# Seven products of quarters in 44 of 76 projections of a two-layer hybrid trunk

## The chip, the cores and the metric

The kernel runs on one core of a Trainium2 chip. The metric is the device time of one execution in microseconds (us); lower is better. Before the change three runs gave 1742.62, 1742.88 and 1743.02 us.

## The reference

Two layers work on x of 512 tokens by 2048 features in float32. Each layer normalises x, projects it with one matrix `w_in` (2048 by 7696), feeds three branches with slices of the projection, and sends the concatenated branches through `w_out` (2048 by 2048) into the residual.

```python
h = _rmsnorm(x, norm_g)
proj = h @ w_in          # 4 x 512 conv, 4 x 1024 attention, 256+256+512+512+16 GLA
y_conv = b_gate * (conv3(c_gate * cv_h) + bias) * silu(cv_g)
# stick-breaking attention, 8 heads of 128, strictly causal
z = q @ k.T              # q, k RMS-normed per head
log_keep = where(mask, log_sigmoid(-z), 0)
later = cumsum(log_keep, reverse=True) - log_keep
w = where(mask, exp(log_sigmoid(z) + later), 0)
y_sb = (w @ v) * silu(sb_g)
# gated linear attention (GLA), 4 heads, decay per key feature
y_gla = _rmsnorm(o, gla_on_g) * silu(gl_g)
return x + concat([y_conv, y_sb, y_gla]) @ w_out
```

## The kernel before

**Products in three terms.** Float32 is carried by pairs of float16: every operand a is split into a high part, float16(a), and a low part, float16(a - high), after scaling by a power of two. A product is high x high + high x low + low x high, accumulated in PSUM. ScalarE (ACT) makes the high parts, VectorE (DVE) the low parts by one scalar-tensor-tensor instruction.

**Groups.** All weights are cut into 76 column groups of 256 (38 per layer; one has 16 columns more), listed in `specs` in the order in which they are used: six for GLA, four for the first half of the convolution, sixteen for attention (V, gate, Q, K for each of four pairs of heads), four for the second half of the convolution, eight for `w_out`. A group is 2048 rows by 256 columns: 16 blocks k of 128 rows.

- Token-major groups (`project_toks`, `tok_mm`, L576 to L578) hold a block of x (128 by 128) stationary and move 256 weight columns: 4 token blocks x 16 k x 3 terms = 192 matmuls. `project_by_token` (L601) does the same work, token block by token block.
- Column-major groups (`project_cols`, L568 to L570) hold 128 weight columns stationary and move 512 tokens: 2 x 16 x 3 = 96 matmuls.

**Weights.** `fetch` (L308) loads a group from DRAM on the SP queue as two staged halves of 1 MB, two groups ahead. Staging has three buffers of half a group. `load_` prepares the next group: a square with a sum on ACT (`wmax`, L319) for its scale, a reduction across partitions on GpSimd and a few tiny DVE instructions (`wscale`, L329 to L350), then the high half on ACT (`whi`, L392) and the low half on DVE (`wlo`, L399), each as two instructions of 2048 elements. For `w_out` a separate scale for each pair of rows makes that four instructions of 512 elements in each half.

**Mix.** Every branch output is split into a high and a low part with a scale of its own as soon as it exists (`mixsplit`, L647 and L648) and stays in SBUF until the output groups; the ratios of the scales are put into the `w_out` weights (`weight_ratio`).

**Attention.** While the projections of one pair of heads run, the scores and values of the pair before are put between them (`later`, `go`). `scores` makes for each head and each of two chunks of 896 and 384 elements: |z|, its exponential and ln(1+e) on ACT (L952 to L954), relu(-z) (L956), then on DVE w = -relu - ln (L958), a = z - w (L959), a reversed running sum of a (L962), w minus the shifted sum (L965), an exponential on ACT (L966), and the float16 pair of the result (L969, L970), which SP transposes by DMA. `values` multiplies by V (L988) and gates the result (L995). `gate` (L611 to L618) computes SiLU with five ACT instructions and two of DVE for each 512 tokens. Q and K are normalised and split by L1033 to L1054 and transposed by DMA.

**Output.** `finish` (L1078) adds the residual, stores the result, and ACT squares it for the next norm (L1084). The last output group goes token block by token block, and `xprep` makes the normalised x of the next layer behind it (L447 to L487).

What sets the order: each engine runs its own queue in order. The order on DVE and ACT at the start is written out by hand; the rest is ordered at build time from the program's order, with raised priority for the loading of weights. PSUM has three banks for projections (`psp`), two double banks for attention and GLA (`psz`) and one more (`psm`).

Of the kernel before, what the change touches and what calls it, by code (L numbers as in the profile page):

```python
# [20 lines left out]
XBITS = 8.0  # L21
# [9 lines left out]
CHUNKS = ((((3, 0), (2, 512)), (3, 2)), (((0, 0), (1, 128)), (0, 1)))  # L31


@with_exitstack
def hybrid_trunk(ctx, tc, x, norm_g, w_in, conv_w, conv_b, sb_qn_g, sb_kn_g,
# [10 lines left out]
    GX = GW + LR  # L46
    NG = D // GW
# [37 lines left out]
    xs = dram.tile([seq, D], F32, tag="xs", name="xs")  # L85
    xt = [newbig("x", [P, 2, D], F32) for _ in range(2)]
# [22 lines left out]
    parno = wk([P, 32], "raw", 1)  # L109
# [162 lines left out]
    specs = []  # L272
    for l in range(depth):
        for cols in ([(GL_V, GW)], [(GL_V + GW, GW), (GL_LR, LR)], [(GL_Q, GW)], [(GL_K, GW)],
                     [(GL_G, GW)], [(GL_G + GW, GW)]):
            specs.append((l, w_in, cols))
        conv = [[(l, w_in, [(c0 + j * GW, GW)]) for c0 in (CV_H, CV_C, CV_G, CV_B)] for j in range(2)]
        specs += conv[0]
        for j in range(4):
            for c0 in (SB_V, SB_G, SB_Q, SB_K):  # L280
                specs.append((l, w_in, [(c0 + j * GW, GW)]))
        specs += conv[1]
        for gi in range(NG):
            specs.append((l, w_out, [(gi * GW, GW)]))
# [10 lines left out]
    def junk(n):  # L295

        return wk([P, HK * GX], "junk", 1, dt=U8)[:, :n]


    def fetch(i):  # L300

        l, src, cols = specs[i]
        staged[i] = st = []
        for h in range(2):
            s_ = stage.tile([P, HK, GX], F32, tag="st", name=nm("st"))
            o = 0
            for c0, w in cols:
                nc.sync.dma_start(  # L308
                    s_[:, :, o:o + w],
                    src[l, h * HK * P:(h + 1) * HK * P, c0:c0 + w].rearrange("(k p) n -> p k n", p=P))  # L310
                o += w
            st.append(s_)

    def wmax(i, h):

        n = sum(c[1] for c in specs[i][2])
        if h == 0:
            peak[i] = sm(2, "wm")
        S.activation(junk(HK * n).rearrange("p (k n) -> p k n", k=HK), staged[i][h][:, :, :n], AF.Square,  # L319
                     accum_out=peak[i][:, h:h + 1])  # L320

    def wscale(i):

        l, src, cols = specs[i]

        m = sm(1, "wq")
        if i:
            gm = sm(2, "wgm")
            G.partition_all_reduce(gm, peak.pop(i), P, RED.add)  # L329
# [14 lines left out]
        sw = None  # L344
        if src is w_out:
            sw = sm(8, "wsr")
            V.tensor_scalar(sw, ratio[l][0], sc, None, ALU.mult)
            V.tensor_tensor(u, p2, ratio[l][1], ALU.mult)
        else:
            V.tensor_tensor(u, p2, xun[:, l:l + 1], ALU.mult)  # L350
        loaded[i] = ([], u)
        scales[i] = (sc, sw)

    def wparts(i, h):
        sc, sw = scales[i]
        return [(slice(2 * j, 2 * j + 2), sw[:, h * 4 + j:h * 4 + j + 1]) for j in range(4)] \
            if sw is not None else [(slice(0, HK), sc)]
# [13 lines left out]

    def whi0(h, q, eng):

        if q == 0:
            wh = wpool.tile([P, HK, GX], F16, tag="wh", name=nm("wh"))
            wl = wpool.tile([P, HK, GX], F16, tag="wl", name=nm("wl"))
            loaded[0][0].append((wh, wl))
# [751 lines left out]
```

## Time and profile before

| | |
|---|---|
| Median of three runs | 1742.88 us |
| Span of the profiled execution | 1740.9 us |
| TensorE matmuls busy | 1726.8 us, 12846 matmuls |
| TensorE weight loads busy | 1232.4 us |
| DVE busy | 1068.9 us, 2015 instructions |
| ACT busy | 1090.0 us, 1460 instructions |
| GpSimd (POOL) busy | 75.1 us, 104 instructions |
| DMA | 204.69 MB, mean 118 GB/s |
| Granted TensorE clock | 1.000 |

The span runs from the first to the last instruction; the execution's own time is not listed apart from the runs, and the span lies 2.0 us under their median. Matmuls overlap, so their busy time says when the engine had work and not how fast it ran; the pace is seen from one start to the next. A row of a group gives line, engine, operation, output and inputs with shapes and the count, then busy us and mean ns of one, then the engine's idle time ahead of these instructions and what ended it. The names in a row are those of the buffers' first users, so that a block of x may stand as `m`.

### The profile page before, as it was taken

What the parts mean: (1) busy time and instruction counts of PE and PEld (TensorE: products, weight loads), DVE (VectorE), ACT (ScalarE), POOL (GpSimd) and SP (SyncE); (2) the same over time, 40 slices, a digit from 0 to 9 for tenths busy, and PEclk for the clock granted to TensorE, in tenths of its full rate; (3) what the DMA queues carried; (4) which work ended last, traced back from release to release, by engine and by line L of the source; (5) the groups of instructions that cost most, each with busy time, mean ns of one, the idle gap of its engine ahead of it and who ended that gap; (6) DMA issues with size and microseconds to landing.
All of it is one profiled execution on the core that took longest, in us unless ns stands there. A gap on an engine that the chain in (4) does not pass through costs nothing.

```text
span 1740.9 us, 30651 instructions
## 1 busy us (share of the span) xinstructions
PE 1726.8 (99%) x12846; PEld 1232.4 (71%) x12846; DVE 1068.9 (61%) x2015; ACT 1090.0 (63%) x1460; POOL 75.1 (4%) x104
## 2 busy tenths in 40 slices
PE   8999999999999999999999999999999999999999
PEld 6744556868787754788885455668686868448888
DVE  7556788657665747433474576976575666673431
ACT  7558577667575867455555684766767667663540
POOL 1000000000000000000010000000000000000000
PEclk9999999999999999999999999999999999999999
DMA  6333313335353545444463333133454444453531
GB/s 222 121 97 97 98 58 113 103 104 131 108 140 110 128 121 128 134 158 146 138 148 105 97 97 97 50 121 110 125 124 109 117 124 126 112 132 113 177 124 40
DMA packets 266121, 204.69 MB, mean 118 GB/s; under 512 B 93106, under 2 KB 265212, under 8 KB 265472
## 3 DMA queue, kind: packets, MB, share of 16 engines
q1 hardware_dynamic: 256976, 193.29, 39.0%
q10 hardware_dynamic: 9008, 9.45, 1.6%
q8 instruction: 100, 1.64, 0.4%
q14 instruction: 37, 0.30, 0.1%
HBM read 173.36 MB, written 8.39 MB: 104 GB/s over the span
## 4 chain that ended last, share of the span: by engine, by line
PE 48%; issue 7%; DVE 1%; DMA 1%; SPq 0%; POOL 0%; ACT 0%; POOLq 0%; DVEq 0%
PE psp L576 8%; PE psp L578 8%; PE psp L577 8%; PE psp L570 6%; PE psp L568 6%; PE psp L569 6%; PE psp L601 3%; PE psz L749 1%; PE psm L988 1%; PE psz L944 1%; PE psz L840 0%; DMA m<-raw 0%; DVE wl L399 0%; SPq L487 0%; DMA xs<-x 0%
## 5 line engine op out<-in xcount | busy, mean ns | idle before, releaser
L577 PE MATMUL psp<-wl,m 128*128 128x256 f16 x1664 | 454.0, 273 | 0.0
L578 PE MATMUL psp<-wh,m 128*128 128x256 f16 x1664 | 453.9, 273 | 0.0
L576 PE MATMUL psp<-wh,m 128*128 128x256 f16 x1664 | 453.8, 273 | 0.0
L399 DVE SCALAR_TENSOR_TENSOR wl<-st,ws,wh 128x2048 f16<-128x2048 f32 (+1 forms) x120 | 282.3, 2353 | 193.1 <-ACT wh L392 179.7
L392 ACT ACTIVATE wh<-st,ws 128x2048 f16<-128x2048 f32 (+1 forms) x118 | 236.3, 2003 | 202.6 <-PE psp L569 100.9
L319 ACT ACTIVATE junk<-st 128x2048 uint8<-128x2048 f32 (+1 forms) x150 | 285.5, 1903 | 7.6 <-DMA st<-in_w_out_dram 4.5
L577 PE MATMUL psp<-wl,x 128*128 128x256 f16 x768 | 209.5, 273 | 0.0
L578 PE MATMUL psp<-wh,x 128*128 128x256 f16 x768 | 209.5, 273 | 0.0
L576 PE MATMUL psp<-wh,x 128*128 128x256 f16 x768 | 209.4, 273 | 0.0
L570 PE MATMUL psp<-m,wl 128*128 128x512 f16 x512 | 194.4, 380 | 0.0
L568 PE MATMUL psp<-x,wh 128*128 128x512 f16 x512 | 194.4, 380 | 0.0
L569 PE MATMUL psp<-x,wh 128*128 128x512 f16 x512 | 194.4, 380 | 0.0
L569 PE MATMUL psp<-m,wh 128*128 128x512 f16 x512 | 194.4, 380 | 0.0
L568 PE MATMUL psp<-m,wh 128*128 128x512 f16 x512 | 194.4, 380 | 0.0
L570 PE MATMUL psp<-x,wl 128*128 128x512 f16 x512 | 194.3, 380 | 0.0
L570 PEld LDWEIGHTS <-wl 128*128 128x128 f16 x1024 | 100.1, 98 | 122.8 <-issue 3.7
L569 PEld LDWEIGHTS <-wh 128*128 128x128 f16 x1024 | 100.1, 98 | 117.5 <-issue 1.1
L568 PEld LDWEIGHTS <-wh 128*128 128x128 f16 x1024 | 100.1, 98 | 115.3 <-issue 0.5
L576 PEld LDWEIGHTS <-m 128*128 128x128 f16 x1664 | 162.7, 98 | 19.9 <-issue 0.7
L578 PEld LDWEIGHTS <-m 128*128 128x128 f16 x1664 | 162.6, 98 | 19.4 <-issue 0.5
L577 PEld LDWEIGHTS <-m 128*128 128x128 f16 x1664 | 162.6, 98 | 18.8
L392 ACT ACTIVATE wh<-st,wsr 128x512 f16<-128x512 f32 x128 | 81.6, 710 | 100.5 <-PE psp L578 74.4
(285 smaller groups left out, 2260.4 us busy)
## 6 DMA issues: line engine op xcount, KB each, us to landing
st<-in_w_in_dram SPq DMA_DIRECT2D x120, 1024.0 KB, 5.3
st<-in_w_out_dram SPq DMA_DIRECT2D x32, 1024.0 KB, 5.5
x<-in_x_dram SPq DMA_DIRECT2D x4, 1024.0 KB
qT<-in_x_dram ACTq DMA_DIRECT2D x8, 512.0 KB, 5.3
qT<-xs ACTq DMA_DIRECT2D x8, 512.0 KB
xs<-x SPq DMA_DIRECT2D x14, 256.0 KB, 4.5
out_dram<-kT SPq DMA_DIRECT2D x14, 256.0 KB, 3.7
th<-za SPq DMA_TRANSPOSE x64, 3.6
```

The lines of the kernel that those rows point to most:

```text
L319: S.activation(junk(HK * n).rearrange("p (k n) -> p k n", k=HK), staged[i][h][:, :, :n], AF.Square, accum_out=peak[i][:, h:h + 1])
L392: lasthi[i] = S.activation(wh[:, ks, :n], staged[i][h][:, ks, :n], AF.Copy, scale=s_)
L399: V.scalar_tensor_tensor(wl[:, ks, :n], staged[i][h][:, ks, :n], s_, wh[:, ks, :n], ALU.mult, ALU.subtract)
L568: T.matmul(o, wh[:, kk, cs], xh[:, :, k, :], start=st_, stop=False)
L569: T.matmul(o, wh[:, kk, cs], xl[:, :, k, :], start=False, stop=False)
L570: T.matmul(o, wl[:, kk, cs], xh[:, :, k, :], start=False, stop=en)
L576: T.matmul(o, ah[:, t, k, :], wh[:, kk, :n], start=st_, stop=False, skip_group_check=True)
L577: T.matmul(o, ah[:, t, k, :], wl[:, kk, :n], start=False, stop=False, skip_group_check=True)
L578: T.matmul(o, al[:, t, k, :], wh[:, kk, :n], start=False, stop=en, skip_group_check=True)
L601: T.matmul(o[:, :n], a_[:, t, k, :], w[k // HK][part][:, k % HK, :n], start=i == 0 and k == 0, stop=i == 2 and k == KT - 1)
L749: T.matmul(o, src16[sb][a][:, ss], tgt16[tb][b][:, g0:g1].rearrange("p g h c -> p (g h c)"), start=i == 0, stop=i == 2)
L944: T.matmul(z[:, o:o + (t + 1) * P], qT[:, a_, t, hh, :], kT[:, b_, :t + 1, hh, :], start=i == 0 and o % 512 == 0, stop=False, skip_group_c ...
```

## The change

Forty-four groups, 22 in each layer, are computed by seven products instead of eight (a form of Strassen's method with shared sums). The 512 tokens are halved, the 2048 rows are halved and the 256 columns are halved: x and the weights become four quarters each, and the four quarters of the result come from seven products of 256 tokens by 1024 rows by 128 columns. The groups are the sixteen of attention, the first of the second conv half, and output groups 2 to 6. All others stay as they were, with weights in quarters of 512 rows.

- **Products.** `seven` runs seven products, each over 8 blocks k and 3 terms: token-major with 2 token blocks and 128 moving columns (48 matmuls), column-major with 256 moving tokens (24 matmuls). Products 0 and 2 share a bank, and so do 4 and 6. Between them ACT copies the bank after product 0 (`s1`), and DVE reads the other after product 4 (`u2`). Three ACT copies and six DVE instructions of 256 elements assemble a projection; an output group takes two copies and about ten DVE instructions with the residual.
- **Weights.** `right` makes seven high and low parts of 1024 elements. Four need sums of quarters: three of these are DMAs on the GpSimd queue that accumulate 512 KB from SBUF into SBUF (`onto`), and one is a DVE subtraction. Staging has four buffers, the finished weights six of a quarter or a product.
- **Sums of x.** At the start of each layer `x_sums` makes four sums of quarters on DVE, splits them, and transposes them with 16 DMAs on SP.
- **Mix.** Branch outputs are written to DRAM in float32 (`spill`), read back into SBUF during the second conv half (`mix_load`), and split with one scale for all (`mix_split`); `mix_sums` makes their sums of quarters. The per-row scales of `w_out` are gone. The float16 pairs of x and of the mix share one pair of tiles.
- **Attention.** A running sum of relu(z) + ln(1+e) is made by one scan with two inputs, and z minus that sum replaces the three DVE instructions around the scan.
- **SiLU.** The gate is exp(-ln(1+exp(-y))) times y: three ACT instructions, a minimum and a product on DVE.

```diff
+SEVEN = {"gla": (), "conv0": (), "sb": (0, 1, 2, 3), "conv1": (0,), "out": (2, 3, 4, 5, 6)}
-    stage = ctx.enter_context(tc.tile_pool(name="stage", bufs=3))
-    wpool = ctx.enter_context(tc.tile_pool(name="wpool", bufs=3))
-    big = ctx.enter_context(tc.tile_pool(name="big", bufs=4))
+    stage = ctx.enter_context(tc.tile_pool(name="stage", bufs=4))
+    wpool = ctx.enter_context(tc.tile_pool(name="wpool", bufs=6))
+    big = ctx.enter_context(tc.tile_pool(name="big", bufs=2))
...
+    def onto(x, y):
+        G.dma_start(out=x, in_=y, accum_op=ALU.add)
+
+    def right(i):
+        a, b = (staged[i][0][:, :, c * P:(c + 1) * P] for c in range(2))
+        c, d = (staged[i][1][:, :, c * P:(c + 1) * P] for c in range(2))
+        def part(x):
+            w = wtile(i)
+            hi, lo = (w[:, h, :HK * P].rearrange("p (k n) -> p k n", n=P) for h in range(2))
+            his.setdefault(i, []).append(S.activation(hi, x, AF.Copy, scale=scales[i]))
+            V.scalar_tensor_tensor(lo, x, scales[i], hi, ALU.mult, ALU.subtract)
+        part(a)
+        part(d)
+        onto(d, b)
+        part(c)
+        part(b)
+        V.tensor_tensor(a, d, a, ALU.subtract)
+        onto(c, d)
+        part(d)
+        part(a)
+        part(c)
...
     def load_(i):
-        with tc.issue_after(lasthi[i - 1].ins):
+        with tc.issue_after(his[i - 1][min(1, len(his[i - 1]) - 1)].ins):
             for h in range(2):
                 wmax(i, h)
+        if modes[i]:
+            onto(*(staged[i][0][:, :, c * P:(c + 1) * P] for c in (1, 0)))
         wscale(i)
...
+    def seven(left, by_cols, evict):
+        w, u = weights()
...
+        o1 = bank(psp, "p")
+        product(o1, 0, True, False)
+        with tc.high_priority():
+            s1 = tmp("s1")
+            S.activation(s1, o1[:, half], AF.Copy, scale=ev.unit)
+        o2 = bank(psp, "p")
+        product(o2, 1, True, True)
+        with tc.high_priority():
+            ev.keep(0, 1, o2[:, half])
+        product(o1, 2, False, True)
+        ev.first(o1[:, half])
+        o3 = bank(psp, "p")
+        product(o3, 3, True, True)
+        o4 = bank(psp, "p")
+        product(o4, 4, True, False)
+        with tc.high_priority():
+            u2 = tmp("u2")
+            ev.add(u2, o4[:, half], s1)
+            ev.sub(u2, o3[:, half], u2)
+        ev.both(0, 1, u2)
+        o5 = bank(psp, "p")
+        product(o5, 5, True, True)
+        with tc.high_priority():
+            y7 = tmp("y7")
+            ev.add(y7, o5[:, half], s1)
+        ev.last4(u2, o5[:, half])
+        product(o4, 6, False, True)
+        ev.plus(1, 0, o4[:, half], y7)
...
+    def x_sums():
+        for t in range(2):
+            column_sums([(xt[0][:, t, :D // 2], xt[0][:, t, D // 2:], xt[1][:, t, :D // 2], xt[1][:, t, D // 2:])])
...
+                        nc.sync.dma_start_transpose(sums[i][hl][:, :, t, :], parts[i, t][:, hl])
...
-                S.activation(y, ps[c], AF.Copy, scale=u)
-                S.activation(a, y, AF.Abs)
-                S.activation(a, a, AF.Exp, scale=-1.0)
-                S.activation(a, a, AF.Ln, bias=1.0)
-                V.scalar_tensor_tensor(a, y, 0.0, a, ALU.min, ALU.subtract)
-                S.activation(a, a, AF.Exp)
-                V.tensor_tensor(y, y, a, ALU.mult)
+                S.activation(a, ps[c], AF.Exp, scale=nu)
+                V.tensor_scalar(a, a, 2.0 ** 62, None, ALU.min)
+                S.activation(a, a, AF.Ln, bias=1.0)
+                S.activation(a, a, AF.Exp, scale=-1.0)
+                V.scalar_tensor_tensor(g[:, c, :], ps[c], u, a, ALU.mult, ALU.mult)
...
-                    S.activation(w, z[:, :zw], AF.Relu, scale=nzun[:, l:l + 1])
-                    V.scalar_tensor_tensor(w, w, -1.0, a, ALU.mult, ALU.subtract)
-                    V.scalar_tensor_tensor(a, z[:, :zw], zs, w, ALU.mult, ALU.subtract)
+                    S.activation(w, z[:, :zw], AF.Relu, scale=zs)
                     for t, o in qtiles:
-                        back = a[:, o:o + (t + 1) * P][:, ::-1]
-                        V.tensor_tensor_scan(back, ones.to_broadcast([P, (t + 1) * P]), back, 0.0,
-                                             ALU.mult, ALU.add)
-                    V.tensor_tensor(w[:, :zw - 1], w[:, :zw - 1], a[:, 1:], ALU.subtract)
+                        grow_, keep_ = (x[:, o:o + (t + 1) * P][:, ::-1] for x in (w, a))
+                        V.tensor_tensor_scan(keep_, grow_, keep_, 0.0, ALU.add, ALU.add)
+                    V.scalar_tensor_tensor(w, z[:, :zw], zs, a, ALU.mult, ALU.subtract)
                     S.activation(w, w, AF.Exp)
...
+        y = conv_in(1, go)
+        m32 = mix_load()
+        s_ = conv_out(1, y, go)
         while later:
             go()
-
+        LATE = (10, 11, 2, 3)
+        for k in (0, 4, 6, 8, 12, 14, 10, 2):
+            mix_split(k, s_)
+        if any(modes[cursor[0]:cursor[0] + NG]):
+            sums = mix_sums(s_)
```

More of the change, by code (lines that the diff above doesn't have):

```diff
@@ L295, in junk @@
     def junk(n):
-        return wk([P, HK * GX], "junk", 1, dt=U8)[:, :n]
+        return wk([P, HK * GW], "junk", 1, dt=U8)[:, :n]
     def fetch(i):
@@ L519, in hybrid_trunk @@
     xlow(0, 1, mix, True)
-    wlo(0, 0)
-    wlo(0, 1)
+    for q in range(4):
+        wlo(0, q)
     xhigh(1, 0, mix)
@@ new lines, in project_by_token, with quarters, own @@
+    def project_by_token(n):
+        w, u = weights()
+        for t in range(NT):
+            o = bank(psp, "p")
+            for i, (a_, part) in enumerate(((xh, 0), (xl, 0), (xh, 1))):
+                for k in range(KT):
+                    T.matmul(o[:, :n], a_[:, k, t, :], wview(w, part, k, n),
+                             start=i == 0 and k == 0, stop=i == 2 and k == KT - 1)
+            yield t, o, u
+    def quarters(sums):
+        def own(th, kh):
+            return [a[:, kh * HK:(kh + 1) * HK, 2 * th:2 * th + 2, :] for a in mix]
+        return own(0, 0), sums[3], own(0, 1), sums[0], sums[1], sums[2], own(1, 1)
```

557 lines of the change are left out of this document (365 added, 192 removed).

## The prediction

> **What bounds the kernel now.** I read the page's busy times and chain first, then the stages by window, then the matmuls' own pace in the timeline, then VectorE (DVE) and ScalarE (ACT) by line in one attention period, and last the DMA issues and the SP queue's waits.
>
> ```profile
> span 1740.9 us, 30651 instructions
> PE 1726.8 (99%) x12846; PEld 1232.4 (71%) x12846; DVE 1068.9 (61%) x2015; ACT 1090.0 (63%) x1460; POOL 75.1 (4%) x104
> 45.00:276.00 231.00, 231.00 (x1416) 130.51 (x1414) 157.81 (x328) 149.09 (x210) 7.70 (x13) 1.00 0.30 94
> 1274.30:1364.90 90.60, 90.60 (x742) 71.27 (x741) 58.88 (x101) 62.57 (x77) 4.62 (x5) 1.00 0.47 121
> 710.00:867.00 157.00, 157.00 (x1440) 140.39 (x1439) 59.10 (x129) 82.43 (x149) 3.19 (x8) 1.00 0.46 148
> ```
>
> The last three rows are the start of a layer, one attention period (four projection groups and two heads, from one head's value matmuls to the same point a period later) and the output groups. Columns: length, then busy PE, weight loads, DVE, ACT and POOL, then the granted clock (1.00) and the DMA share. TensorE never stops in any of them, and DVE and ACT have a third free. So TensorE's instruction stream is the time, and a saving there counts until another engine fills up.
>
> ```profile
> 419.74 0.27 PE L576 MATMUL psp<-wh,x 128*128 128x256 f16 x1
> 422.91 0.27 PE L578 MATMUL psp<-wh,x 128*128 128x256 f16 x1
> 639.71 0.38 PE L568 MATMUL psp<-x,wh 128*128 128x512 f16 x1
> 641.44 0.38 PE L570 MATMUL psp<-x,wl 128*128 128x512 f16 x1
> 157.77 1.54 PEld L749 LDWEIGHTS <-m 128*128 128x128 f16 x24
> 157.98 1.50 PE L749 MATMUL psz<-m 128*128 128x128 f16 x24
> 159.32 0.38 PE L568 MATMUL psp<-x,wh 128*128 128x512 f16 x1
> 1160.34 3.32 PE psz L840 x48
> ```
>
> Durations of matmuls overlap, so pace is start to start. Between the first two rows lie 29 steps, so 3.17/29 = 0.1093 us for 256 columns; the next two lie 8 steps apart, 1.73/8 = 0.216 us for 512. The run of 24 matmuls with 128 columns, each with a load of its own, took 159.32 - 157.98 = 1.34 us: 0.0558 each. The last row confirms this: 36 of 128 columns and 12 of 256 make 36 x 0.0558 + 12 x 0.1093 = 3.32. So halving the columns does halve the time, weight loads included, which is what the change stands on.
>
> **TensorE's part.** A token-major group is 192 matmuls of 256 columns, 20.99 us. By seven products it is 7 x 48 of 128 columns, 336 x 0.0558 = 18.75 us: 2.24 less. A column-major group is 96 x 0.216 = 20.76 us and becomes 7 x 24 of 256 columns, 168 x 0.1093 = 18.36: 2.40 less. Of the 44 groups 34 are token-major (per layer V, Q and K of four periods, and five output groups) and 10 column-major (four gates and the first of conv half 1). That is 34 x 2.24 + 10 x 2.40 = 100.2 us. If nothing else stood in the way the span would be 1640.7.
>
> **The attention periods.** Eight periods, each with three token-major groups and one column-major group: PE falls by 3 x 2.24 + 2.40 = 9.1 to 81.5 us. Does DVE fit in it?
>
> ```profile
> L399 DVE SCALAR_TENSOR_TENSOR wl<-st,ws,wh 128x2048 f16<-128x2048 f32 x8 | 18.8, 2350 | 15.8 <-ACT wh L392 15.8
> L1054 DVE SCALAR_TENSOR_TENSOR qp<-raw,qp 128x1024 f16<-128x1024 f32 x2 | 2.5, 1225 | 2.2 <-ACT qp L1053 2.2
> L958 DVE SCALAR_TENSOR_TENSOR zw<-zw,za 128x896 f32<-128x896 f32 x2 | 2.2, 1092 | 5.2 <-ACT za L954 5.2
> L965 DVE TENSOR_TENSOR zw<-zw,za 128x895 f32<-128x895 f32 x2 | 2.2, 1078 | 0.0
> L995 DVE SCALAR_TENSOR_TENSOR e<-psm,vu,g 128x256 f32<-128x256 f32 x4 | 1.7, 477 | 0.0
> L648 DVE SCALAR_TENSOR_TENSOR m<-e,bsmix,m 128x512 f16<-128x512 f32 x2 | 1.5, 752 | 0.0
> L616 DVE SCALAR_TENSOR_TENSOR ga<-g,ga 128x512 f32<-128x512 f32 x2 | 1.4, 688 | 0.9 <-ACT ga L615 0.9
> L965 DVE TENSOR_TENSOR zw<-zw,za 128x383 f32<-128x383 f32 x2 | 1.1, 554 | 0.0
> L958 DVE SCALAR_TENSOR_TENSOR zw<-zw,za 128x384 f32<-128x384 f32 x2 | 1.1, 552 | 0.0
> L735 DVE TENSOR_TENSOR m<-e,m 128x256 f16<-128x256 f32 x32 | 13.4, 423 | 7.8 <-ACT m L734 7.3
> L856 DVE TENSOR_SCALAR e<-e 128x512 f32<-128x512 f32 x8 | 3.4, 426 | 0.1
> ```
>
> The first nine rows are DVE's groups in the period quoted above (busy us, mean ns, then idle before them and its releaser); the last two are of the whole span. The low halves of the weights cost 18.8. In their place stand seven parts of 1024 elements and one subtraction of 1024 per group, at the 1.23 of the form of L1054: 4 x 8 x 1.23 = 39.4. Each seven-product group evicts with six DVE instructions of 256 elements, between the 0.42 of L735 and the 0.48 of L995: 4 x 6 x 0.45 = 10.8. Gone are L958 and L965 (3.3 + 3.3; the scan keeps its length and adds two operands instead of scaling one, taken as equal) and the mix's low half, 1.5; the gate's minimum costs 0.43 for 0.69, so 0.5 less. DVE: 58.9 - 18.8 + 39.4 + 10.8 - 6.6 - 1.5 - 0.5 = 81.7 us. It meets PE's 81.5.
>
> DVE can't be full all the time. Its idle time before the low halves (15.8) becomes work, but 5.2 + 2.2 + 0.9 = 8.3 us were waits for ACT inside the attention and gate chains, which stay. Bounds are none of it and all of it; I take half, since other groups' parts can fill some: 81.7 + 4.1 = 85.8 us a period. Gain 90.6 - 85.8 = 4.8, times 8: **38 us** of the 73 that PE offers.
>
> ```profile
> L392 ACT ACTIVATE wh<-st,ws 128x2048 f16<-128x2048 f32 x8 | 16.0, 1998 | 15.3 <-PE psp L578 11.0 <-PE psp L569 4.3
> L319 ACT ACTIVATE junk<-st 128x2048 uint8<-128x2048 f32 x8 | 15.2, 1900 | 0.1
> L1033 ACT ACTIVATE raw<-psp 128x512 f32<-128x512 f32 x4 | 2.3, 576 | 0.0
> L1053 ACT ACTIVATE qp<-raw 128x1024 f16<-128x1024 f32 x2 | 2.1, 1057 | 5.6 <-DVE raw L1049 3.3 <-DVE raw L1044 2.3
> L647 ACT ACTIVATE m<-e,bsmix 128x512 f16<-128x512 f32 x2 | 1.4, 722 | 4.1 <-DVE e L995 4.1
> L613 ACT ACTIVATE ga<-g 128x512 f32<-128x512 f32 x2 | 1.3, 638 | 0.0
> L734 ACT ACTIVATE m<-e 128x256 f16<-128x256 f32 x32 | 12.9, 408 | 19.0 <-PE psz L749 12.8 <-DVE e L773 6.0
> L1078 DVE SCALAR_TENSOR_TENSOR x<-psp,wu,qT 128x512 f32<-128x512 f32 x14 | 10.5, 751 | 51.0 <-PE psp L578 51.0
> ```
>
> ACT in the same period: 62.6 - 16.0 + 28 parts x 1.06 (29.6) - 1.4 - 2.3 - 2.6 (the SiLU loses two of five activations on two halves, 4 x 0.64) + 12 eviction copies of 256 x 0.41 (4.9) = 74.8, nine tenths of the period. It fits, without being free.
>
> **Output groups and conv half 1.** Here DVE has room: a seven-product output group needs 9.8 of weights and about ten 256-element evictions, 4.5, in 18.75. Ten groups save 10 x 2.24 = **22 us**, the two conv groups **5 us**.
>
> **What is added at the layer's seams.** After the last conv group DVE must make four mix pairs (4 x 1.23 = 4.9), eight sums and eight low halves (16 x 1.23 = 19.7), the weights of output groups 1 and 2 (4.9 + 9.8, 1.7 of scales) and four evictions of 0.75 (L1078): 44 us, before the second product of output group 2, 2 x 20.99 + 2.68 = 44.7 us later. That just fits, so the cover is thin: I charge 3 us a layer, **6 us**; bounds are nothing and all 19.7 twice. The sums of x (16 x 1.23 = 19.7 on DVE each layer, and 16 transposing DMAs on SP ahead of later weight fetches) go into a stretch of 231 us in which DVE is idle for 73: nothing; uncovered they would cost 2 x 19.7. The mix's way through DRAM is read back over the last three conv groups, 60 us, and the shorter SiLU and removed memsets lie off PE's stream: nothing.
>
> **The accumulating DMAs.** They are in no trace of this kernel, and three of them in a row stand in each group's weight path. Staging holds two groups, so a pair of buffers is held for the landing of two halves, the squares, three accumulations of T each and the last part.
>
> ```profile
> st<-in_w_in_dram SPq DMA_DIRECT2D x120, 1024.0 KB, 5.3
> qT<-in_x_dram ACTq DMA_DIRECT2D x8, 512.0 KB, 5.3
> q10 hardware_dynamic: 9008, 9.45, 1.6%
> SPq L308 <- DVE wl L399: 975.6, 121, 20.5
> ```
>
> The last row says that the weight fetch already waits on SP for a staging buffer to come free, 121 times, and SP's transposes for attention stand behind it. The hold is 2 x 5.3 + 2.1 (L319 with its read-out) + 3T + 2.3 (one part on ACT, one on DVE) = 15.0 + 3T, and a group can't be faster than half of it. For T the nearest row is a plain 512 KB load, 5.3 us to landing; an accumulation also reads its destination, so twice that, 10.6, is the other end. A smaller T gains nothing. I take 5.3: half the hold is 15.5 us, inside the 18.75. The engines' own time: q10 moved eighteen such 512 KB loads in 1.6% of the span, 1.55 us each; twelve accumulations cost 19 to 37 us a period beside the 0.47 x 90.6 = 42.6 there, a share of 0.75 to 0.98 of 81.5. That stays under one, barely at the upper end. The Trainium skill (DMA: Bandwidth & Descriptors, Anatomy of one DMA) fits a transfer from the GpSimd queue as 2.0 us plus its bytes over 436 GB/s; by that T would be an estimated 3.2 us and the sum the same.
>
> **Sum.** 1740.9 - 38 - 22 - 5 + 6 = 1682 us of span. The median shown is 1742.9, 2 us above this span; so **1684 us**.
>
> **Rivals.**
>
> *The waits fill up.* If DVE's 8.3 us are all covered by parts of other groups, the periods come to 81.7 and the time to 1684 - 8 x 4.1 = 1651. For it: the weight work is due only within a window of five products. Against: both engines would have to run at 100% in order. Chance 0.17.
>
> *PE waits in mid-group (slower).* In each seven-product group product 2 continues the bank that ACT must have copied after product 0, and product 6 the bank that DVE must have read after product 4: one product (2.68 us) of time, 88 places, where before PE waited for an eviction only between groups. ACT, at nine tenths, serves in order, and an L319 of 1.9 us or a few parts may stand ahead. The point is 58/88 = 0.66 us each; at half an L319, 0.95, the time is 1684 + 84 = 1768. For it: fill of both engines. Against: these copies are given priority. Chance 0.19.
>
> *Accumulations are slow (slower).* Staging takes over when (15.0 + 3T)/2 passes 18.75, T = 7.5, and in the periods the gain is lost at T = 10.1, where the half hold is 90.6/4. At T = 10.6 a group takes 23.4: 8 x (93.6 - 85.8) + 10 x 4.7 + 2 x 5.0 = 119 more, 1803 us. Its place is POOL's queue: each accumulation waits there for parts on ACT and DVE, and the next weight scale's reduction stands behind. The Trainium skill (SBUF — State Buffer, Who interferes with whom) would add that GpSimd can't write descriptors while DVE runs a two-port instruction; the only such long one that I see added is the gate's minimum, whose row beside the two-input forms (0.43 against 0.69) looks like that mode, so by that rule T grows by under half a us, twice per gate. Chance 0.15.
>
> *The seven products save nothing.* If 128-column matmuls alternating stationaries held a slower pace than the two dense runs above, the point is 20.99/336 = 0.0625 each. Both runs contradict that; it lies in the 0.03 for no change.
>
> **Numbers.** The forecast itself (1664 to 1725) has 0.43, the first rival 0.17, a gain smaller than either 0.03, no change 0.03, slower 0.34. No change means within 0.2%, 3.5 us, about what can be told apart. So faster 0.63, same 0.03, slower 0.34. The range runs from 1648, just under the first rival, to 1790, past the second and most of the third.
>
> **What would show it.** PE starts 0.056 us apart in the products with 128 columns. An attention period near 86 us with DVE over 90% busy; if it is near 82, the waits were filled; if over 90, look at what PE's products wait for: ACT's copy or DVE's first sum (second rival), or weight parts behind an accumulation (third), whose landing time is to be read from the DMA issues. Output groups should come 18.8 us apart, with no PE gap over 5 us ahead of output group 2. The forecast is wrong if DVE has idle time in the periods while PE waits.

## The result: slower by 15%, and the profile after

The changed kernel takes 2004.56 us (median; 2003.47 to 2009.21), the kernel before 1742.95 us in the same comparison: a ratio of 1.1507, 95% interval 1.1491 to 1.1523. The forecast was 1684 us, and the time lies far above its range.

First the page of the changed kernel: span, busy times, granted clock, the DMA share by slice, the accumulations' queue, the chain that ended last, the costliest groups (busy us, mean ns | idle before them, releaser) and the issues (KB each, us to landing).

```profile
span 2003.5 us, 43388 instructions
PE 1724.3 (86%) x18462; PEld 1370.9 (68%) x18462; DVE 1383.2 (69%) x2521; ACT 1253.4 (63%) x1696; POOL 275.3 (14%) x236
PEclk9999989998888889998899899989998889899999
DMA  6823365999989997379877324559999999974993
q0 software_dynamic: 137280, 69.21, 32.8%
DMA 15%; issue 12%; PE 11%; DVE 7%; ACT 2%; POOL 1%; SPq 1%; POOLq 0%; DVEq 0%; ACTq 0%
L429 ACT ACTIVATE w<-st,ws 128x1024 f16<-128x1024 f32 x308 | 349.8, 1142 | 278.4 <-DMA st<-st 246.8
L430 DVE SCALAR_TENSOR_TENSOR w<-st,ws,w 128x1024 f16<-128x1024 f32 x308 | 392.9, 1280 | 150.9 <-ACT w L429 150.6
L419 POOL DMA_DIRECT2D st<-st x132 | 207.2, 1722 | 969.3 <-DVE w L430 257.9
L437 DVE TENSOR_TENSOR st<-st,st 128x1024 f32<-128x1024 f32 x44 | 53.9, 1226 | 173.0 <-DMA st<-st 173.0
st<-st POOLq DMA_DIRECT2D x132, 512.0 KB, 8.0
```

TensorE (PE) was busy for 99% of the span and is now at 86%, with a lower granted clock; DVE is at 69%. So no engine is full over the whole span. The row of DMA has nines where attention runs, twice, and again near the end. The queue that carries the accumulations did not exist before; it takes 32.8% of 16 engines' span, 0.328 x 2003.5 / 132 = 4.98 us of all sixteen for each accumulation of 512 KB, and one lands 8.0 us after its issue (the median). ACT stands idle for these sums ahead of its weight parts (L429) for 246.8 us, DVE ahead of its subtraction (L437) for 173.0 us.

To see where the time went, the same event is followed through each kernel: the DVE maximum of V, once in each attention period. The rows are from the timeline by line, layer 1 and layer 2: duration in ns (min/median/max), then the first and the last start in us. Three periods lie between the two. Before, after, and the changed kernel without its accumulations (experiment 1):

```profile
L1013 DVE TENSOR_REDUCE bm<-v x4: 1208/1209/1210, 283.2 to 557.7; 128x1 f32<-128x1024 f16 x4
L1013 DVE TENSOR_REDUCE bm<-v x4: 1209/1210/1210, 1140.5 to 1415.0; 128x1 f32<-128x1024 f16 x4
```

```profile
L1241 DVE TENSOR_REDUCE bm<-v x4: 1212/1215/1220, 323.2 to 662.9; 128x1 f32<-128x1024 f16 x4
L1241 DVE TENSOR_REDUCE bm<-v x4: 1212/1216/1218, 1330.9 to 1666.8; 128x1 f32<-128x1024 f16 x4
```

```profile
L1241 DVE TENSOR_REDUCE bm<-v x4: 1209/1211/1214, 314.0 to 562.3; 128x1 f32<-128x1024 f16 x4
L1241 DVE TENSOR_REDUCE bm<-v x4: 1210/1211/1214, 1161.5 to 1410.2; 128x1 f32<-128x1024 f16 x4
```

With the spans (1740.9, 2003.5 and 1721.5 us) the differences of these starts cut the time in five:

| stretch, us | before | after | without accumulations |
|---|---|---|---|
| start to the first V | 283.2 | 323.2 | 314.0 |
| three periods, layer 1 | 274.5 | 339.7 | 248.3 |
| last period, second conv half, output, start of layer 2 | 582.8 | 668.0 | 599.2 |
| three periods, layer 2 | 274.5 | 335.9 | 248.7 |
| last period to the end | 325.9 | 336.7 | 311.3 |

Half of the loss against before (65.2 + 61.4 of 262.6 us) lies in six attention periods. The third stretch holds another of them, and the output groups. They take 113 us each where 91.5 stood and 85.8 was forecast. The windows over the three periods of layer 1, before and after (length, then busy PE, weight loads, DVE, ACT, POOL, granted clock, DMA share, GB/s):

```profile
283.20:557.70 274.50, 274.50 (x2244) 215.35 (x2243) 175.73 (x308) 185.15 (x227) 11.25 (x15) 1.00 0.43 114
```

```profile
323.20:662.90 339.70, 269.49 (x3713) 252.40 (x3710) 231.79 (x408) 212.82 (x279) 67.30 (x51) 0.90 0.96 155
```

DVE is busy for 231.79 of 339.70 us and PE for 269.49: this is the sign that the prediction named against itself, DVE idle while PE waits. The DMA share went from 0.43 to 0.96, while the bytes rose only from 114 to 155 GB/s. Per period the DMA engines are busy for 0.96 x 113.2 = 109 us, against 81.5 us of PE's work. That alone does not make them the limit: the share adds up the times of packets, and a share near 1 isn't the most that it reaches. Between 60 and 90 us, in the same run, it is 1.08, with more bytes per second:

```profile
60.00:90.00 30.00, 27.88 (x228) 22.17 (x227) 18.73 (x50) 17.39 (x22) 4.03 (x4) 0.99 1.08 223
```

The waits of the changed kernel show what that does (engine, line and what it waited for: us in total, times, longest):

```profile
ACT w L429 <- DMA st<-st: 246.8, 67, 7.7
POOL st L419 <- DMA st<-st: 227.6, 40, 9.9
DVE st L437 <- DMA st<-st: 173.0, 43, 8.2
PE psm L1215 <- DMA th<-za: 65.8, 18, 9.9
```

The last row is collateral: the transposed attention weights come by DMA too, and PE waited 65.8 us for them (5.7 us in experiment 1, which leaves the accumulations out). And because each engine runs its queue in order, other work stands behind a wait. In the timeline of DVE and of ACT around 1308 us (start, us, what, then the idle time before it and its releaser):

```profile
1307.65 1.23 DVE L437 TENSOR_TENSOR st<-st,st 128x1024 f32<-128x1024 f32 x1 [4.56 <-DMA st<-st]
1308.91 0.42 DVE L940 TENSOR_TENSOR th<-qT,th 64x256 f16<-64x256 f32 x1
1309.36 0.43 DVE L975 SCALAR_TENSOR_TENSOR e<-e,qT 128x256 f32<-128x256 f32 x1
1309.82 0.85 ACT L939 ACTIVATE th<-e 64x256 f16<-64x256 f32 x2 [7.55 <-DVE e L975]
```

DVE idles 4.56 us for an accumulation; GLA's L940 and L975 follow it; ACT, which needs L975, has idled 7.55. The chain that ended last alternates in the same way, in layer 2 (start, us, what):

```profile
1391.80 11.98 DMA st<-st
1403.81 0.19 POOL wgm L345
1404.00 12.86 issue
1416.87 10.53 DMA st<-st
1427.45 0.04 issue
1427.50 1.23 DVE st L437
```

### The profile page after: what moved, and what is told of

Its sections match the earlier page's. It is cut to its first block, busy times and chain, and to the rows that moved or that the text cites. A ratio compares the mean times of both kernels' runs of the same rounds, so it can differ in the third digit from the quotient of the medians.

```text
span 2003.5 us, 43388 instructions
## 1 busy us (share of the span) xinstructions
PE 1724.3 (86%) x18462; PEld 1370.9 (68%) x18462; DVE 1383.2 (69%) x2521; ACT 1253.4 (63%) x1696; POOL 275.3 (14%) x236
## 3 DMA queue, kind: packets, MB, share of 16 engines
q0 software_dynamic: 137280, 69.21, 32.8%
## 5 line engine op out<-in xcount | busy, mean ns | idle before, releaser
L429 ACT ACTIVATE w<-st,ws 128x1024 f16<-128x1024 f32 x308 | 349.8, 1142 | 278.4 <-DMA st<-st 246.8
L430 DVE SCALAR_TENSOR_TENSOR w<-st,ws,w 128x1024 f16<-128x1024 f32 x308 | 392.9, 1280 | 150.9 <-ACT w L429 150.6
L670 PE MATMUL psp<-w,act 128*128 128x128 f16 x4896 | 326.0, 233 | 54.1 <-ACT s L682 22.8
L670 PEld LDWEIGHTS <-act 128*128 128x128 f16 x4896 | 315.6, 106 | 76.7 <-issue 62.0
L419 POOL DMA_DIRECT2D st<-st x132 | 207.2, 1722 | 969.3 <-DVE w L430 257.9
L332 ACT ACTIVATE junk<-st 128x2048 uint8<-128x2048 f32 x150 | 285.5, 1903 | 67.4 <-DMA st<-in_w_in_dram 50.2
L670 PEld LDWEIGHTS <-s 128*128 128x128 f16 x4608 | 270.6, 100 | 23.1 <-issue 21.6
L670 PE MATMUL psp<-w,s 128*128 128x128 f16 x4608 | 278.7, 223 | 0.9 <-ACT raw L734 0.9
L616 PE MATMUL psp<-act,w 128*128 128x512 f16 x704 | 267.8, 380 | 0.0
L615 PE MATMUL psp<-act,w 128*128 128x512 f16 x704 | 267.8, 380 | 0.0
L617 PE MATMUL psp<-act,w 128*128 128x512 f16 x704 | 267.6, 380 | 0.0
L412 DVE SCALAR_TENSOR_TENSOR w<-st,ws,w 128x1024 f16<-128x1024 f32 x128 | 162.7, 1280 | 55.5 <-ACT w L408 53.0
L667 PEld LDWEIGHTS <-w 128*128 128x128 f16 x1680 | 167.3, 100 | 42.4 <-DVE u L719 13.3
L408 ACT ACTIVATE w<-st,ws 128x1024 f16<-128x1024 f32 x124 | 139.6, 1140 | 65.0 <-PE psp L617 50.5
L437 DVE TENSOR_TENSOR st<-st,st 128x1024 f32<-128x1024 f32 x44 | 53.9, 1226 | 173.0 <-DMA st<-st 173.0
L643 PEld LDWEIGHTS <-act 128*128 128x128 f16 x1152 | 114.4, 100 | 32.3 <-issue 9.2
L615 PEld LDWEIGHTS <-w 128*128 128x128 f16 x704 | 69.1, 98 | 83.1 <-issue 3.9
L616 PEld LDWEIGHTS <-w 128*128 128x128 f16 x704 | 69.0, 98 | 83.2 <-issue 4.6
L617 PEld LDWEIGHTS <-w 128*128 128x128 f16 x704 | 69.1, 98 | 81.8 <-issue 1.8
```

Of the source, the lines that this page charges most:

```text
L332: S.activation(junk(HK * GW).rearrange("p (k n) -> p k n", k=HK), staged[i][h], AF.Square, accum_out=peak[i][:, h:h + 1])
L408: his.setdefault(i, []).append(S.activation(quarter(i, q, 0)[:, :, :GW], staged4(i, q), AF.Copy, scale=scales[i]))
L412: V.scalar_tensor_tensor(lo[:, :, :GW], staged4(i, q), scales[i], hi[:, :, :GW], ALU.mult, ALU.subtract)
L419: G.dma_start(out=x, in_=y, accum_op=ALU.add)
L429: his.setdefault(i, []).append(S.activation(hi, x, AF.Copy, scale=scales[i]))
L430: V.scalar_tensor_tensor(lo, x, scales[i], hi, ALU.mult, ALU.subtract)
```

## The experiments

The theory after the result: the accumulating DMAs cost the whole loss, and without them the change gains. Rivals: PE waits in mid-group for its evictions (the prediction's second rival), or the rest of the change (sums, mix, attention, SiLU) is what costs.

**1. No accumulations.**

```diff
     def onto(x, y):
-        G.dma_start(out=x, in_=y, accum_op=ALU.add)
+        return
```

> Leaves out the 132 accumulating DMAs, so four of the seven weight parts are made of unsummed quarters; everything else runs as in the changed kernel. Theory A (the accumulations hold up the staging and the in-order ACT and DVE queues, and TensorE and its clock wait for that): at least 220 of the 262 us go, 1690 to 1780 us, granted clock back to 0.98 or more. Theory B (PE's waits in mid-group, ACT and DVE too full): the accumulations are hidden anyway, 1900 us or more. Theory C (the seams: sums of x, mix through DRAM, shared tiles): some 60 to 100 us above the forecast remain, 1745 to 1800.

Measured: 1723.09 us, ratio 0.9889 (0.9869 to 0.9909). One full period of layer 2 by window, then the largest of the waits in mid-group:

```profile
1242.34:1325.63 83.29, 81.78 (x1242) 78.01 (x1240) 77.75 (x139) 73.02 (x99) 2.04 (x5) 1.00 0.52 135
```

```profile
PE psp L670 <- DVE u L716: 7.5, 10, 1.3
```

So the accumulations cost 281 us, more than the whole loss, and the rest gains 20. PE waits 7.5 us in all at L670 for DVE's sums in mid-group, and 1.1 us for ACT's copy: the second rival is out. A period takes 83.3 us with PE at 81.78 and DVE at 77.75.

**2. All 44 groups as before, the rest of the change kept.**

```diff
-SEVEN = {"gla": (), "conv0": (), "sb": (0, 1, 2, 3), "conv1": (0,), "out": (2, 3, 4, 5, 6)}
+SEVEN = {"gla": (), "conv0": (), "sb": (), "conv1": (), "out": ()}
```

> No group by seven products, so no sums of x or of the mix and no accumulation; the rest of the change stays (mix through DRAM with one scale, one running sum, shorter SiLU, quarters of weights, more staging). Forecast and theory A: off TensorE's stream, 1743 within 10 us, and 1735 at best. Theory C: the 28 us that each layer's start lost are from these parts, 1780 to 1820 us.

Measured: 1745.74 us, ratio 1.0019 (1.0009 to 1.0028). Attention from one sum, the shorter SiLU, one scale and the mix in DRAM together gain nothing and cost about 3 us (1.6 to 4.9 by the interval). Sums are not made here, so this says nothing on them.

**3. The sums by DVE.**

```diff
-        G.dma_start(out=x, in_=y, accum_op=ALU.add)
+        V.tensor_tensor(x, x, y, ALU.add)
```

> The three accumulations of a group become three DVE additions of 1024 elements (1.23 us each), same results. Theory A: DVE goes from 81.7 to 96.5 us a period, about 100 with its waits; 1684 + 8 x 14.8 = 1800, 1780 to 1840 us, far under 2004. Theory B: DVE is the bound already, so 132 x 1.23 = 162 us come on top: 2050 to 2170.

Measured: 1802.69 us, ratio 1.0346 (1.0325 to 1.0366).

```profile
321.50:599.70 278.20, 258.17 (x3779) 242.75 (x3777) 265.36 (x438) 212.73 (x280) 17.82 (x15) 0.99 0.44 118
```

```profile
L419 DVE TENSOR_TENSOR st<-st 128x1024 f32<-128x1024 f32 x88 | 107.1, 1217 | 4.5 <-ACT junk L332 4.5
```

DVE is busy for 265.36 of 278.20 us: it is the bound. That the time lies so near the computed 1800 is luck in part: the period came out at 92.7 us and not at 96.5 to 100, while 38 us more than before are lost ahead of the first V (321.5 for 283.2). Even so this is 202 us better than the DMAs, which were there to spare DVE.

**4. The sums by GpSimd.**

```diff
-        G.dma_start(out=x, in_=y, accum_op=ALU.add)
+        G.tensor_tensor(x, x, y, ALU.add)
```

> The three accumulations become three GpSimd additions of 1024 elements, same results. Theory A: if one takes up to 3 us, it is well under the 8.0 us that an accumulation took to land, and the time is 1690 to 1800 us. Theory B: no change from 2004. If GpSimd's reads of SBUF hold up DVE's two-input instructions, DVE's low halves get longer than 1.28 us and the time stays above 1850.

Measured: 2069.35 us, ratio 1.1876 (1.1852 to 1.19), the slowest of all. The groups of this run:

```profile
L430 DVE SCALAR_TENSOR_TENSOR w<-st,ws,w 128x1024 f16<-128x1024 f32 x308 | 440.9, 1436 | 112.9 <-ACT w L429 112.1
L437 DVE TENSOR_TENSOR st<-st,st 128x1024 f32<-128x1024 f32 x44 | 104.1, 2367 | 36.6 <-POOL st L419 36.6
L1282 DVE SCALAR_TENSOR_TENSOR qp<-raw,qp 128x1024 f16<-128x1024 f32 x16 | 28.5, 1782 | 4.0 <-ACT qp L1281 4.0
L419 POOL TENSOR_TENSOR st<-st,st 128x1024 f32<-128x1024 f32 x44 | 117.2, 2664 | 328.2 <-issue 245.4
```

An addition takes GpSimd 2.7 us, and DVE's instructions with two operands in SBUF grow beside it: L437 from 1226 to 2367 ns, L430 from 1280 to 1436, L1282 from 1219 to 1782. The Trainium skill (SBUF — State Buffer, Who interferes with whom) says that a DVE instruction with two SBUF inputs contends with a GpSimd instruction that reads SBUF; these rows agree and give it a size. How much of the loss is the additions themselves, how much the longer DVE instructions and how much the order on GpSimd (experiment 6) was not separated.

**5. The same transfers without adding.**

```diff
-        G.dma_start(out=x, in_=y, accum_op=ALU.add)
+        G.dma_start(out=x, in_=y)
```

> The three transfers of a group stay on the GpSimd queue with the same bytes, places and waits, but copy instead of adding, so the sums of weights are not made. If the adding is what makes them slow: landing falls from 8.0 us to the 5.3 of a plain 512 KB load, their share of the DMA engines from 33% to about 12% (1.55 us each), and the time is 1730 to 1800 us. If it is the queue, the descriptors and three transfers in a row: landing stays at 7 to 8 us and the time above 1930.

Measured: 1805.76 us, ratio 1.0366 (1.0346 to 1.0387), just above the range expected.

```profile
q0 software_dynamic: 19008, 69.21, 14.0%
st<-st POOLq DMA_DIRECT2D x132, 512.0 KB, 5.0
```

```profile
312.10:591.30 279.20, 255.10 (x3711) 241.19 (x3709) 230.61 (x409) 211.11 (x277) 40.05 (x51) 0.96 0.73 187
```

Between the same addresses a copy is 144 packets (19008/132), takes 0.14 x 1805.7 / 132 = 1.92 us of the sixteen engines and lands in 5.0 us; adding makes that 1040 packets, 4.98 and 8.0. The copy's figures are near the 5.3 us that the prediction took and inside its 1.55 to 3.1 us: those are prices of a copy. So 199 of the 281 us are what adding costs, and 83 remain for three copies in a row in each group's path.

**6. Order on GpSimd.** In the changed kernel a group's first accumulation stands in GpSimd's queue ahead of the last one of the group before, whose parts are needed first. Here it waits for that.

```diff
     def onto(x, y):
-        G.dma_start(out=x, in_=y, accum_op=ALU.add)
+        last_onto.append(G.dma_start(out=x, in_=y, accum_op=ALU.add))
...
         if modes[i]:
-            onto(*(staged[i][0][:, :, c * P:(c + 1) * P] for c in (1, 0)))
+            ab = [staged[i][0][:, :, c * P:(c + 1) * P] for c in (1, 0)]
+            if last_onto:
+                with tc.issue_after(last_onto[-1].ins):
+                    onto(*ab)
+            else:
+                onto(*ab)
```

> The same accumulations, but the first of a group is issued behind the last of the group before; in the changed kernel it stands ahead of it on POOL's queue, so that a group's last weight part waits for the next group's landing and squares. If that order is what stretches the chain: 1850 to 1930 us. If the accumulations' own time is: within 30 us of 2004.

Measured: 1962.85 us, ratio 1.1268 (1.1246 to 1.1291), between the two expectations: the order is worth 42 us and not the rest. GpSimd's waits for ACT's squares ahead of an accumulation fell from 243.6 to 93.2 us.

```profile
319.90:640.90 321.00, 262.91 (x3714) 246.98 (x3712) 230.22 (x409) 213.57 (x282) 67.46 (x51) 0.92 0.99 162
```

The period fell from 113.2 to 107.0 us, with the DMA engines now at a share of 0.99. That fits a limit by the engines' time and doesn't show one, since the share can pass 1.

**7. Each quarter of the weights as one run of memory.** The staged quarters are rows of 512 bytes, 128 columns out of 256. Here the fetch lays each quarter down as one run of 4 KB in a partition; the accumulations stay.

```diff
+            if modes[i]:
+                s_ = s_.rearrange("p k n -> p (k n)").rearrange("p (c k n) -> p c k n", c=2, n=P)
+                for c in range(2):
+                    nc.sync.dma_start(s_[:, c], src[l, h * HK * P:(h + 1) * HK * P, c0 + c * P:c0 + (c + 1) * P]
+                                      .rearrange("(k p) n -> p k n", p=P))
...
-        a, b = (staged[i][0][:, :, c * P:(c + 1) * P] for c in range(2))
-        c, d = (staged[i][1][:, :, c * P:(c + 1) * P] for c in range(2))
+        a, b = (staged[i][0][:, c].rearrange("p k n -> p (k n)") for c in range(2))
+        c, d = (staged[i][1][:, c].rearrange("p k n -> p (k n)") for c in range(2))
```

> The changed kernel with each weight quarter staged as one run of 4 KB per partition instead of eight of 512 bytes (the fetch goes in two DMAs per half, in runs of 512 bytes); accumulations as in the change. If the accumulations are slow by their number of pieces (1040 packets each against 144 for a plain copy): landing falls from 8.0 to 5 to 6 us, 1800 to 1880 us. If by the bytes that are added: landing stays at 7.5 to 8 us, 1970 to 2010. ACT's and DVE's parts of 1.14 and 1.28 us should fall to the 1.06 and 1.23 of unbroken rows in either case.

Measured: 1892.35 us, ratio 1.0865 (1.0841 to 1.0888).

```profile
q0 software_dynamic: 19008, 69.21, 20.3%
st<-st POOLq DMA_DIRECT2D x132, 512.0 KB, 5.7
L435 ACT ACTIVATE w<-st,ws 128x1024 f16<-128x1024 f32 x308 | 349.6, 1142 | 131.4 <-DMA st<-st 84.7
```

```profile
317.20:614.10 296.90, 264.23 (x3719) 246.34 (x3717) 232.12 (x411) 212.80 (x279) 39.46 (x51) 0.93 0.86 178
```

144 packets again, 0.203 x 1887.7 / 132 = 2.90 us of the engines, and 5.7 to landing, as expected; 112 us come back, with the same bytes and the same sums. The time is just above its range. Landing and engines' time fell together here, so this run doesn't tell which of the two gave the 112 us. One expectation missed: the weight parts did not get shorter (1142 ns on ACT, as before), so the broken rows are not why they take more than the 1057 ns of L1053. That they take their scale from a tensor and not as a constant is argued only.

**8. Both.** Contiguous quarters and the order of experiment 6; the diff is the sum of the two.

> The contiguous staging of the experiment before and the order on GpSimd of the earlier one together: a quarter of a weight group is one 4 KB run per partition, and a group's first accumulation is issued only after the last one of the group ahead. Theory E (in the changed kernel the 16 DMA engines are full in the attention periods: share 0.96 of 113 us, 0.99 of 107 us once the order was mended, so the order could bring the period down only to the engines' own 106 us): with 4 KB runs the engines need 0.86 x 99 = 85 us a period, so now the order is free to bring more than the 6 us it brought before: periods of 88 to 93 us with a DMA share above 0.9, time 1790 to 1845 us. Rival F (the order cost time only because each landing took 8 us and stood in front of the next; at 5.7 us it costs little): periods stay at 96 to 100 us, time 1865 to 1895. In both the landing stays at 5.5 to 6 us.

Measured: 1834.72 us, ratio 1.0533 (1.0502 to 1.0563).

```profile
314.20:598.10 283.90, 253.08 (x3717) 239.54 (x3714) 228.78 (x409) 211.43 (x279) 43.27 (x51) 0.96 0.89 183
```

The order is now worth 58 us, more than the 42 that it was worth with the DMA engines at 0.99, and the time falls in the first theory's range; the period (94.6 us, 96.0 in layer 2) fell between the two theories' ranges, and the share (0.89) just short of 0.9. That the order is worth more once the engines need less time speaks for their time as one limit, though not the only one; the landings are shorter here too, so it isn't shown apart.

The periods of layer 1 side by side; the last column is the DMA share times the period, a sum of packets' times and no lower bound of the period:

| kernel | total, us | a period, us | DMA share | DMA engines' time in it, us |
|---|---|---|---|---|
| changed | 2004.6 | 113.2 | 0.96 | 109 |
| order | 1962.9 | 107.0 | 0.99 | 106 |
| contiguous | 1892.4 | 99.0 | 0.86 | 85 |
| contiguous and order | 1834.7 | 94.6 | 0.89 | 84 |
| copy without adding | 1805.8 | 93.1 | 0.73 | 68 |
| DVE adds | 1802.7 | 92.7 | 0.44 | 41 |

**9. Output groups alone, sums by DVE.** Where DVE has room, do the seven products bring what was forecast?

```diff
-SEVEN = {"gla": (), "conv0": (), "sb": (0, 1, 2, 3), "conv1": (0,), "out": (2, 3, 4, 5, 6)}
+SEVEN = {"gla": (), "conv0": (), "sb": (), "conv1": (), "out": (2, 3, 4, 5, 6)}
...
-        G.dma_start(out=x, in_=y, accum_op=ALU.add)
+        V.tensor_tensor(x, x, y, ALU.add)
```

> Only the ten output groups by seven products, weight sums by DVE additions, no sums of x. DVE has 9.8 + 3.7 + 4.5 = 18.0 us of work in a group of 18.75. From the run without any seven-product group, 1745.7, less 10 x 2.24, plus 3 us a layer for the mix's sums: 1729 us, 1722 to 1738. If the sums of the mix are not covered, up to 39 more: above 1743.

Measured: 1740.17 us (1737.91 to 1745.16), ratio 0.9991 (0.9981 to 1.0000). That lies between the two expectations, 5.6 us under experiment 2, where the forecast has 22 less a seam of 6. It is the best version with all sums made, and a tie with before.

**10. The sums of x.** As experiment 9, with the first group of the second conv half by seven products as well, which alone brings the sums of x in at the start of each layer.

```diff
-SEVEN = {..., "conv1": (), "out": (2, 3, 4, 5, 6)}
+SEVEN = {..., "conv1": (0,), "out": (2, 3, 4, 5, 6)}
```

> Like the run with only the output groups (1740.2 us), plus the first group of conv half 1 in each layer by seven products, which needs the sums of x at each layer's start; weight sums by DVE. If the sums of x are covered, as forecast: two groups save 4.8, 1735 us, 1732 to 1739. If they hold up the first groups of a layer (in the run without accumulations Q's first maximum came 14 us later in layer 1, and the gap between the layers grew by about as much): 1758 to 1768 us.

Measured: 1760.30 us (1758.85 to 1761.51), ratio 1.0105 (1.0088 to 1.0121): 20 us more than experiment 9, though two groups more got shorter. The window from 30 to 60 us of experiment 9, then of this one:

```profile
30.00:60.00 30.00, 27.89 (x249) 24.30 (x247) 26.39 (x86) 24.84 (x35) 3.38 (x5) 1.00 0.45 140
```

```profile
30.00:60.00 30.00, 19.63 (x147) 16.44 (x145) 28.82 (x63) 21.90 (x29) 1.16 (x3) 0.85 0.29 79
```

DVE was already busy for 26.39 of 30 us. The sums fill it to 28.82, and PE drops from 27.89 to 19.63: in this window it waits 5.5 us for DVE's low part of x (L512) and 4.6 us for a weight part of ACT (L408). The maximum of V shows what is left of that at its first start, again for experiment 9 and then for this one:

```profile
L1241 DVE TENSOR_REDUCE bm<-v x4: 1207/1207/1209, 287.5 to 559.1; 128x1 f32<-128x1024 f16 x4
```

```profile
L1241 DVE TENSOR_REDUCE bm<-v x4: 1207/1210/1210, 301.4 to 573.8; 128x1 f32<-128x1024 f16 x4
```

The first V comes 13.9 us later, and the periods behind it take the same.

**11. The sums of x later.** Experiment 1 with `sums = x_sums()` moved behind GLA's first groups in the program.

```diff
-        sums = x_sums() if any(modes[cursor[0]:cursor[0] + 30]) else None
+        seven_in = any(modes[cursor[0]:cursor[0] + 30])
...
+        sums = x_sums() if seven_in else None
```

> Leaves out the accumulations like the first run (1723.1 us), and makes the sums of x behind the two V groups of GLA instead of at the layer's start. If the sums of x at the start hold up the evictions of the first groups: 1685 to 1703 us. If the loss at the layer's start (14 us before Q's maximum and 18 behind it) comes from elsewhere: within 8 us of 1723.

Measured: 1723.52 us, ratio 0.9894 (0.9874 to 0.9914), no change. DVE is at 29.56 of the 30 us in the same window and still makes the sums there: the order at build time hardly moved. This says nothing on a truly later place.

**12. Two of the four attention groups (V and Q), sums by DVE.** The expectation below has the sums of x behind GLA's V groups; the kernel makes them at the layer's start, as in the change.

```diff
-SEVEN = {..., "sb": (0, 1, 2, 3), ...}
+SEVEN = {..., "sb": (0, 2), ...}
...
-        G.dma_start(out=x, in_=y, accum_op=ALU.add)
+        V.tensor_tensor(x, x, y, ALU.add)
```

> Weight sums by DVE, sums of x behind GLA's V groups, and of each attention period only V and Q by seven products. DVE is left with 50.3 + 2 x 15.2 - 2 x 4.7 + 2 x 2.7 = 76.7 us a period against PE's 90.6 - 4.5 = 86.1, so the period is PE's: 86 to 88 us, 8 x 3.5 less than the output-only run, plus what the sums of x cost: 1735 to 1765. If DVE's fill were not what stretched the periods of the run with all four (92.6 us), they would stay above 90 and the time above 1775.

Measured: 1758.63 us, ratio 1.0097 (1.0077 to 1.0117). Its periods take 86.4 and 87.0 us, 5 less than before; that is 29 us in six periods, yet the time is above that of before. Its first V comes at 318.8 us, 35.6 later than before, and that alone outweighs the 29.

## Why the prediction was wrong, step by step

- **The accumulating DMAs: the step that failed.** Taken: T = 5.3 us by a plain 512 KB load, to be hidden up to 7.5; measured 8.0, and 4.98 us of the sixteen engines where 1.55 to 3.1 was the bound. Both figures were prices of a copy (experiment 5: 5.0 and 1.92); the nearest row had the right bytes but not the right operation. Left out, the accumulations give back 281 us (experiment 1). The Trainium skill (DMA: Bandwidth & Descriptors, Anatomy of one DMA) gave an estimated 3.2 us for T; the trace, with other transfers beside it, doesn't agree, nor for the copy.
- **The third rival was the right one, at a wrong price.** Its chance was 0.15 and its worst 1803 us. Its staging formula gives (15.0 + 3 x 8.0)/2 = 19.5 us a group, 78 a period, which PE's 81.5 would have hidden; measured are 113. The other bound in the same part, the engines' share, was computed as 0.75 to 0.98 and passed over as "under one": its own sum with the measured 4.98 us gives 42.6 + 12 x 4.98 = 102 us, 1.26 of 81.5, and the measured 109 us are 1.33. Both T and the share were too low, and which of them sets the period isn't shown. Missing too was what queues up: the two in-order engines that wait (420 us together), GpSimd's order (42 us), the transposes behind the transfers, and the clock, granted at 0.90 in the periods and at 1.00 where the gaps are gone (experiment 1).
- **The sums of x at nothing: the second step that failed.** DVE's 73 idle us were an average over 231. The sums run ahead of nearly all of that, between 30 and 60 us, where DVE is at nine tenths without them (experiment 10): the first V comes 13.9 us later, and it is 20 us in all, or about 25 if the two shorter groups saved the 5 forecast; that lies between nothing and the 39 named as uncovered.
- **Output groups: 22 less 6 forecast, 5.6 measured.** Which wait took the rest was not settled.
- **The attention periods: better than forecast once the DMAs are gone.** 82.8 us a period for 85.8, six periods 52 us shorter. DVE has 77.75 us for 81.7 forecast, ACT 73.02 for 74.8, PE 81.78 for 81.5: DVE was 4 us too high, so PE bounds the period and its waits fill, as in the first rival. That run still took 1723 and not 1684: it reaches its first V 30.8 us later than before. Of these, 4.3 us stand in experiment 2 already (287.5 us), 13.9 are the sums of x, and 12.6 come on top where the attention groups too go by seven products (314.0 for 301.4 in experiment 10). PE waits there at GLA's L945 for ACT and DVE, 9.3 us up to the first V for 0.6 in experiment 10; what holds these two up was not tested apart.
- **Right:** PE's pace. In the changed kernel's chain the 288 matmuls of 128 columns below make 0.0564 us each (0.0558 forecast). DVE's price of an instruction with two inputs of 1024 elements: 1.23 us taken, 1.22 measured for an addition (experiment 3), though the weights' low parts took 1.28. Attention, SiLU and the mix at nearly nothing (experiment 2). The products' evictions in mid-group not being a bound (experiment 1).

```profile
1962.56 16.24 PE psp L670 x288
```

Open: why copies, or contiguous accumulations in order, still cost 83 and 112 us beside none at all. With a DMA share of 0.73 and 0.89 it is hardly the engines' time alone; three transfers with parts of ACT and DVE between them stand in a row in each group, but more staging, or sums made in another order, wasn't tried.

## What to carry to other kernels

An operation that no trace shows is priced by its kind and not by its bytes: where the nearest row is a copy and the operation reads, adds and writes back, carry the bound until it breaks the schedule and give that case a chance to match. Add up the DMA engines' time per period as for any other engine; a share "barely under one" computed from bounds leaves no room for a wrong price. And look for cover in the very stretch where the added work is due (30 us here), not in the mean of a long stage.

## What the runs showed of the hardware

An accumulation between the same addresses takes 1040 packets and 4.98 us of the 16 DMA engines where a copy takes 144 and 1.92; laid out in 4 KB runs the accumulation too takes 144 packets, and 2.90 us. Over the 512-byte rows its issue holds GpSimd longer than a copy's as well (0.89 us in 4 KB runs), by the timeline of the line that issues them (ns, min/median/max), in the changed kernel and then as a copy:

```profile
L419 POOL DMA_DIRECT2D st<-st x132: 1546/1573/2266, 225.6 to 1958.9; - x132
```

```profile
L419 POOL DMA_DIRECT2D st<-st x132: 882/884/1053, 224.9 to 1761.6; - x132
```
